# The low half of the weights formed by an accumulating DMA in a two-layer hybrid encoder

## The chip, the cores and the metric

The kernel runs on one core of one Trainium2 chip. The time is the device time in microseconds from the first to the last instruction of one execution. Three runs of the kernel before gave 1634.25, 1635.59 and 1636.38 us; the median is 1635.59.

## What is computed

The reference runs two layers on x of 512 tokens and 1024 channels, all in float32. Cut to its matrix products, one layer is:

```python
h = rmsnorm(x, norm1_g[l])
u = h @ w_in[l]                     # q, k, v, glu_in (two halves), four_in
...
y_a = att.reshape(b, s, WIDTH_A) @ w_proj_a[l]       # differential attention, 8 heads
y_b = jax.nn.silu(cv) @ w_proj_b[l]                  # depthwise convolution of width 31
y_c = fr.reshape(b, s, WIDTH_C) @ w_proj_c[l]        # real part of a 2-D DFT
gates = jax.nn.sigmoid(h @ w_gate[l] + b_gate[l]).reshape(b, s, N_BRANCH, d)
merged = gates[:, :, 0] * y_a + gates[:, :, 1] * y_b + gates[:, :, 2] * y_c
x = x + merged @ w_out[l]
h2 = rmsnorm(x, norm2_g[l])
f_gate, f_up = jnp.split(h2 @ w_ffn_in[l], 2, axis=-1)
x = x + (jax.nn.silu(f_gate) * f_up) @ w_ffn_out[l]
```

## The kernel before

All activations lie with channels on the partitions and the 512 tokens along the row, as tiles of 128 x 512. TensorE multiplies in float32r, a rounded form of float32. To keep the precision, both operands are split into a rounded high half and a low half, the rest that the rounding leaves. A product of a weight tile and an activation tile is then three matmuls: high weight by high activation, high weight by low activation, low weight by high activation (`gemm`, which calls `mm` on line 114, where every matmul is recorded). `split` (from line 144) makes the halves of activations: ScalarE rounds (line 147, or line 150 with a scale), VectorE subtracts (line 148 or 151).

The weights of a layer lie in HBM in the order of their use, cut into 134 chunks of 128 x 1024 (eight tiles of 128 x 128, 512 KB), 268 chunks for both layers. `wtile` hands out one tile after another and calls `chunk` (line 185) for every eighth. `chunk` does the following, all with an early due time (`WL`), so that the scheduler puts it ahead of the work that needs it:

- SyncE loads the chunk into a tile `wr` (line 191), of which there are two buffers;
- ScalarE rounds it into `wh` (line 194), three buffers;
- VectorE subtracts `wh` from `wr` into `wl` (line 195), three buffers.

A scheduler orders the instructions of each engine at build time by these due times and by its own estimate of when each can run; each engine then works through its own list in that order, and semaphores make it wait. An instruction that waits holds up all that stands behind it on its engine. A chunk feeds eight times three matmuls, or in the attention's projections (`qkv`) two steps of four token tiles by three matmuls, where it is the wide operand.

Work that shares the engines with the weights: the convolution on VectorE (line 867, 30 of 31 taps of each of four tiles of a layer), whose tiles GpSimd adds up (line 898, three sums per layer); sums of squares for the norms (ScalarE line 236, GpSimd line 239); the attention's scores (maximum on VectorE line 689, exponential on ScalarE line 691); the merge of the branches (GpSimd line 453); and three loads of DFT tables that GpSimd issues (line 340). The last stage of each layer is the feed-forward part, whose products follow one another without attention between them.

Of the kernel before, what the change touches and what calls it, by code (L numbers as in the profile page):

```python
# [9 lines left out]
F32 = mybir.dt.float32  # L10
F32R = mybir.dt.float32r
I32 = mybir.dt.int32
AF = mybir.ActivationFunctionType
ALU = mybir.AluOpType
# [67 lines left out]
class Hybrid:  # L82
# [102 lines left out]
    def chunk(self, l, c, t):  # L185
        nc = self.nc
        tc = self.tc
        keep = tc.cur_priority
        self.at(t - WL)
        raw = self.wp.tile([P, CHUNK * P], F32, tag="raw", name=self.nm("wr"), bufs=WB[0])  # L190
        nc.sync.dma_start(raw, self.a["w"][l, c])
        hi = self.wp.tile([P, CHUNK * P], F32R, tag="hi", name=self.nm("wh"), bufs=WB[1])
        lo = self.wp.tile([P, CHUNK * P], F32R, tag="lo", name=self.nm("wl"), bufs=WB[2])
        nc.scalar.copy(hi, raw)  # L194
        nc.vector.tensor_tensor(out=lo, in0=raw, in1=hi.bitcast(F32), op=ALU.subtract)  # L195
        tc.cur_priority = keep
        return hi, lo

# [865 lines left out]
```

## Time and profile before

| What | Value |
|---|---|
| median of three runs | 1635.59 us |
| profiled execution, its span | 1635.0 us |
| TensorE busy | 1618.7 us (99%) |
| VectorE busy | 1089.5 us (67%) |
| ScalarE busy | 678.2 us (41%) |
| GpSimd busy | 119.5 us (7%) |
| mean granted TensorE clock | 0.998 |
| read from HBM | 163.30 MB |

The profile is of one execution. Engines are named PE (TensorE), PEld (its loading of the stationary operand), DVE (VectorE), ACT (ScalarE), POOL (GpSimd) and SP (SyncE). A group's row gives line, engine, operation, what it writes from what it reads (buffer numbers left out), shapes and count, then the busy time in us, the mean ns of one, and the idle time of the engine just before, with what ended it. A row of the waits reads: engine and line, what it waited for, us in total, times, longest. A row of the timeline begins with start and duration in us. A row of a window gives its length and each engine's busy time in it. A row of the DMA issues ends with KB each and the median us from issue to landing.

The work is uneven: VectorE is busy nine tenths or more of most of the first 330 us, in which the first layer's convolution and scores run, and about four tenths in the feed-forward stages. TensorE is nearly full everywhere after the first 25 us.

### The profile page before, as it was taken

Reading aid. Unit: us, or ns where it says so; the run is one execution under the profiler, and the core shown is the slowest. Engines: PE = TensorE matmul, PEld = TensorE weight load, DVE = VectorE, ACT = ScalarE, POOL = GpSimd, SP = SyncE. Lnnn points to the kernel's source line nnn. Section 1 sums busy time; section 2 is a strip of 40 time slices with the busy share of each in tenths; the row PEclk is TensorE's granted clock in tenths of the full one; section 3 lists DMA queues with packets and bytes.
Section 4 is the critical chain, followed back from the end, with each engine's and each line's share of the span. In section 5 each row is a group of like instructions: output and inputs, shape, how many; then the busy total and the mean of one; then the engine's idle time right before and its main releaser. Section 6 shows DMA issues by size and latency. Waiting matters only on the chain.

```text
span 1635.0 us, 20023 instructions
## 1 busy us (share of the span) xinstructions
PE 1618.7 (99%) x7512; PEld 1340.8 (82%) x7512; DVE 1089.5 (67%) x1820; ACT 678.2 (41%) x1059; POOL 119.5 (7%) x85
## 2 busy tenths in 40 slices
PE   8999999999999999999999999999999999999999
PEld 6888888887888888888888888888878888888887
DVE  7999999896644433444459999998975444334432
ACT  5345555773443221323344464557634332223221
POOL 4000000112410000000100000001132000000000
PEclk9999999999999999999999999999999999999999
DMA  5545233322432323223343542332224223222332
GB/s 177 176 136 165 78 110 102 98 88 71 136 112 94 103 91 100 93 96 104 128 138 95 162 148 81 100 113 85 87 86 146 95 99 102 92 95 99 93 113 77
DMA packets 61439, 178.50 MB, mean 109 GB/s; under 512 B 8976, under 2 KB 9872, under 8 KB 61344
## 3 DMA queue, kind: packets, MB, share of 16 engines
q1 hardware_dynamic: 60912, 176.11, 33.3%
q0 software_dynamic: 432, 1.13, 0.3%
q8 instruction: 59, 0.97, 0.3%
q14 instruction: 36, 0.29, 0.1%
HBM read 163.30 MB, written 13.89 MB: 108 GB/s over the span
## 4 chain that ended last, share of the span: by engine, by line
PE 96%; ACT 2%; DVE 1%; DMA 0%; issue 0%; SPq 0%; DVEq 0%; ACTq 0%
PE main L114 83%; PE s L114 5%; PE att L114 3%; PE oth L114 3%; PE att L124 2%; DMA V<-in_xT 0%; PE att L583 0%; ACT at L691 0%; ACT cv L924 0%; DVE wl L195 0%; PE oth L124 0%; ACT wh L194 0%; DVE B L151 0%; ACT L924 0%; ACT L441 0%
## 5 line engine op out<-in xcount | busy, mean ns | idle before, releaser
L114 PE MATMUL main<-X,wh 128*128 128x512 f32 x2208 | 692.2, 391 | 0.0
L194 ACT CAST wh<-wr 128x1024 fp32r<-128x1024 f32 x268 | 281.7, 1052 | 649.5 <-PE main L114 375.6
L114 PEld LDWEIGHTS main<-X,wh 128*128 128x128 f32 x2208 | 413.4, 188 | 85.1 <-issue 0.5
L195 DVE TENSOR_TENSOR wl<-wr,wh 128x1024 fp32r<-128x1024 f32 x268 | 341.4, 1274 | 139.4 <-ACT wh L194 138.6
L114 PE MATMUL main<-X,wl 128*128 128x512 f32 x1104 | 431.7, 391 | 0.0
L114 PEld LDWEIGHTS main<-X,wl 128*128 128x128 f32 x1104 | 207.5, 188 | 42.7 <-issue 0.5
L867 DVE SCALAR_TENSOR_TENSOR cv<-cv,hcw,cv 128x497 f32<-128x497 f32 (+14 forms) x240 | 176.4, 735 | 1.2
L114 PE MATMUL main<-att,wh 128*128 128x512 f32 x384 | 119.6, 391 | 3.0 <-ACT att L147 3.0
L691 ACT ACTIVATE at<-s,mx 128x512 f32<-128x512 f32 x128 | 88.0, 688 | 78.6 <-DVE mx L689 63.0
L404 DVE TENSOR_TENSOR M<-main,rb 128x512 f32<-128x512 f32 x42 | 29.1, 692 | 133.8 <-PE main L114 133.8
L114 PE MATMUL main<-A,wh 128*128 128x512 f32 x320 | 106.4, 392 | 0.0
L114 PE MATMUL main<-wh,X 128*128 128x512 f32 x288 | 96.5, 391 | 0.0
L401 DVE TENSOR_TENSOR M<-main,rb 128x512 f32<-128x512 f32 x42 | 29.0, 691 | 91.0 <-PE main L114 91.0
L689 DVE TENSOR_REDUCE mx<-s 128x1 f32<-128x512 f32 x128 | 86.5, 679 | 4.3 <-PE s L114 4.0
L114 PEld LDWEIGHTS main<-att,wh 128*128 128x128 f32 x384 | 71.8, 188 | 19.2 <-ACT att L147 3.5
L114 PE MATMUL main<-act,wh 128*128 128x512 f32 x256 | 80.2, 394 | 0.0
L114 PE MATMUL main<-cv,wh 128*128 128x512 f32 x240 | 77.3, 392 | 1.1 <-ACT cv L147 1.1
L239 POOL TENSOR_TENSOR M<-M,M 128x512 f32<-128x512 f32 x28 | 46.9, 1675 | 421.0 <-ACT M L236 378.3
L114 PE MATMUL main<-att,wl 128*128 128x512 f32 x192 | 75.0, 391 | 0.0
L114 PE MATMUL main<-A,wl 128*128 128x512 f32 x192 | 74.9, 392 | 0.0
L114 PEld LDWEIGHTS main<-A,wh 128*128 128x128 f32 x320 | 59.8, 188 | 12.6 <-issue 0.5
L426 DVE TENSOR_TENSOR V<-main,V 128x512 f32<-128x512 f32 x32 | 22.1, 691 | 65.9 <-PE main L114 65.9
(223 smaller groups left out, 2260.9 us busy)
## 6 DMA issues: line engine op xcount, KB each, us to landing
wr<-in_w SPq DMA_DIRECT2D x268, 512.0 KB, 3.5
dqk<-at SPq DMA_DIRECT2D x32, 256.0 KB, 3.8
qst<-dqk SPq DMA_DIRECT2D x96, 64.0 KB, 1.9
kst<-dqk SPq DMA_DIRECT2D x96, 64.0 KB, 1.9
V<-in_xT SPq DMA_DIRECT2D x8, 256.0 KB, 7.6
att<-dftd SPq DMA_DIRECT2D x8, 256.0 KB, 4.2
M<-in_xT SPq DMA_DIRECT2D x8, 256.0 KB, 3.5
x<-V SPq DMA_DIRECT2D x8, 256.0 KB, 2.6
```

The lines of the kernel that those rows point to most:

```text
L114: return self.pin(self.nc.tensor.matmul(out, lhsT=lhsT, rhs=rhs, start=start, stop=stop))
L124: self.pin(self.nc.tensor.transpose(ps[:, s], src[:, s], self.ident))
L194: nc.scalar.copy(hi, raw)
L195: nc.vector.tensor_tensor(out=lo, in0=raw, in1=hi.bitcast(F32), op=ALU.subtract)
L239: nc.gpsimd.tensor_tensor(out=sq, in0=acc, in1=sq, op=ALU.add)
L401: nc.vector.tensor_tensor(out=z, in0=pg, in1=rb2, op=ALU.mult)
L404: nc.vector.tensor_tensor(out=u, in0=pu, in1=rb2, op=ALU.mult)
L426: nc.vector.tensor_tensor(out=x2[m], in0=ps, in1=x2[m], op=ALU.add)
L689: nc.vector.tensor_reduce(out=mx, in_=ps, axis=AX.X, op=ALU.max, negate=True)
L691: nc.scalar.activation(e, ps, AF.Exp, bias=mx, accum_out=z1 if c else z0)
L867: ins = nc.vector.scalar_tensor_tensor(out=acc[:, a:b], in0=g[:, a + d : b + d], scalar=w[:, t : t + 1], in1=acc[:, a:b], op0=ALU.mult, op ...
```

## The change

The low half no longer comes from a subtraction. ScalarE writes the negated weights into `wl`, rounded by the tile's type, and then GpSimd issues a DMA that reads the same chunk from HBM a second time and adds it onto `wl`. What results is the raw value less its rounded form, as before. ScalarE's rounding into `wh` stays. Lines below 193 keep their numbers, those behind it are one higher: the negation is line 194, the DMA 195, the rounding 196.

```diff
         hi = self.wp.tile([P, CHUNK * P], F32R, tag="hi", name=self.nm("wh"), bufs=WB[1])
         lo = self.wp.tile([P, CHUNK * P], F32R, tag="lo", name=self.nm("wl"), bufs=WB[2])
+        nc.scalar.activation(lo, raw, AF.Copy, scale=-1.0)
+        nc.gpsimd.dma_start(lo, self.a["w"][l, c], accum_op=ALU.add)
         nc.scalar.copy(hi, raw)
-        nc.vector.tensor_tensor(out=lo, in0=raw, in1=hi.bitcast(F32), op=ALU.subtract)
         tc.cur_priority = keep
         return hi, lo
```

The scheduler makes new lists of it. Three places matter below. The first is the start of TensorE's list, the first products of the first layer. A_131 and B_132 are the high and low half of the first activation tile, A_137 and B_138 those of the second; wh_193 and wl_194 are the first chunk, wh_225 and wl_226 the second (wh_224 before). Before:

```order
L114 MATMUL s_190<-A_131,wh_193 128x512
L114 MATMUL s_190<-B_132,wh_193 128x512
L114 MATMUL s_190<-A_131,wl_194 128x512
L114 MATMUL s_190<-A_137,wh_193 128x512
L114 MATMUL s_190<-B_138,wh_193 128x512
L114 MATMUL s_190<-A_137,wl_194 128x512
```

With the change:

```order
L114 MATMUL s_190<-A_131,wh_193 128x512
L114 MATMUL s_190<-B_132,wh_193 128x512
L114 MATMUL s_222<-A_131,wh_225 128x512
L114 MATMUL s_222<-B_132,wh_225 128x512
L114 MATMUL s_190<-A_131,wl_194 128x512
L114 MATMUL s_190<-A_137,wh_193 128x512
L114 MATMUL s_190<-B_138,wh_193 128x512
L114 MATMUL s_190<-A_137,wl_194 128x512
```

Two products with the second chunk's rounded half moved ahead of the first product with a low half.

The second place is GpSimd's list around the sums of the convolution in the first layer. Before, nothing stands between the table loads and the sums:

```order
L340 DMA at_512<-in_dft 128x256
L340 DMA at_522<-in_dft 128x512
L340 DMA at_532<-in_dft 128x512
L898 TENSOR_TENSOR cv_2540<-cv_555,cv_876 128x512
L898 TENSOR_TENSOR cv_2542<-cv_2540,cv_1326 128x512
L898 TENSOR_TENSOR cv_2544<-cv_2542,cv_2056 128x512
```

With the change, from the two chunks ahead of the first sum:

```order
L195 DMA wl_2174<-in_w 128x1024
L195 DMA wl_2244<-in_w 128x1024
L899 TENSOR_TENSOR cv_2573<-cv_564,cv_891 128x512
L899 TENSOR_TENSOR cv_2575<-cv_2573,cv_1347 128x512
L195 DMA wl_2382<-in_w 128x1024
L195 DMA wl_2464<-in_w 128x1024
```

The low halves now share one list with the sums, and a low half behind a sum is issued only after it. At the start of the program the first low half stands ahead of the seven sums of squares (line 240), the second behind three of them, the third behind six and the fourth behind all seven.

The third place is ScalarE's list in the feed-forward part, where the silu (line 402 before) and the rounding of activations (line 147) stand between the chunks. Before:

```order
L194 CAST wh_6099<-wr_6097 128x1024
L402 ACTIVATE M_6056<-M_6056 128x512
L194 CAST wh_6140<-wr_6138 128x1024
L147 CAST act_6062<-M_6059 128x512
L194 CAST wh_6171<-wr_6169 128x1024
```

With the change, at a like stretch:

```order
L196 CAST wh_6431<-wr_6429 128x1024
L194 ACTIVATE wl_6432<-wr_6429 128x1024
L403 ACTIVATE M_6386<-M_6386 128x512
L196 CAST wh_6473<-wr_6471 128x1024
L194 ACTIVATE wl_6474<-wr_6471 128x1024
L147 CAST qst_6392<-M_6389 128x512
L196 CAST wh_6505<-wr_6503 128x1024
L194 ACTIVATE wl_6506<-wr_6503 128x1024
```

The negation stands right behind the rounding of the same chunk. Of the 268 chunks, 241 have this order and 27 the other, negation first; those lie at the start of the program and in the attention's projections of both layers.

TensorE's list of the projections hardly moved: between the last product of wl_632 (the eleventh chunk) and the first of wl_831 (the fourteenth) stand 32 matmuls, and as many between the same chunks before; in the feed-forward part two chunks and two matmuls, 50, lie between.

## The prediction

> **What bounds the kernel now.** I read the page first, for the busy time of each engine.
>
> ```profile
> span 1635.0 us, 20023 instructions
> PE 1618.7 (99%) x7512; PEld 1340.8 (82%) x7512; DVE 1089.5 (67%) x1820; ACT 678.2 (41%) x1059; POOL 119.5 (7%) x85
> ```
>
> TensorE leaves 1635.0 - 1618.7 = 16.3 us of the span unused, so a change that touches no matmul can win at most that. The profiled execution's span of 1635.0 stands 0.6 us under the median of the runs, 1635.59; I carry that 0.6 over. The waits of TensorE say whether the step that is removed ever stood in its way (us in total, times, longest):
>
> ```profile
> PE s L114 <- ACT wh L194: 3.0, 1, 3.0
> PE s L114 <- DVE B L151: 2.3, 2, 1.5
> PEld s L114 <- DVE wl L195: 1.3, 2, 0.8
> ```
>
> The first matmul waits once for a rounded half; the low half is waited for twice, 1.3 us together. Both belong to the start of the program. From there on the low half comes early, and the chain of work that ended last shows it: its longest piece is TensorE alone.
>
> ```profile
> 1281.95 349.40 PE main L114 x1535
> ```
>
> That is 349.40 / 1535 = 0.2276 us per matmul, and 24 matmuls = 5.46 us per chunk of weights. So the question is not what VectorE saves but whether a low half that takes a longer way still arrives in time.
>
> **What goes and what comes.** The two operations per chunk now, 268 of each:
>
> ```profile
> L194 ACT CAST wh<-wr 128x1024 fp32r<-128x1024 f32 x268 | 281.7, 1052 | 649.5 <-PE main L114 375.6 <-issue 200.6 <-PE oth L114 45.6
> L195 DVE TENSOR_TENSOR wl<-wr,wh 128x1024 fp32r<-128x1024 f32 x268 | 341.4, 1274 | 139.4 <-ACT wh L194 138.6
> L147 ACT CAST wth<-att 128x512 fp32r<-128x512 f32 x64 | 37.5, 586 | 40.5 <-PE att L124 40.4
> L150 ACT ACTIVATE A<-V,par 128x512 fp32r<-128x512 f32 x16 | 11.5, 716 | 16.6 <-DVE V L426 14.8 <-DMA V<-in_xT 1.7
> ```
>
> VectorE loses 341.4 us (1089.5 to about 748). Of that only the 1.3 us above lay on TensorE's path, so its worth is at most 1.3 us. ScalarE gains a negating ACTIVATE per chunk. A scaled ACTIVATE costs 716 - 586 = 0.13 us more than a CAST of the same 512 columns, so I take 1.052 + 0.1 = 1.15 us, and 268 x 1.15 = 308 us on top of 678. Its densest stretch has room:
>
> ```profile
> 41.00:164.00 123.00, 123.00 (x583) 102.53 (x583) 117.81 (x242) 59.64 (x99) 0.54 (x1) 1.00 0.49 158
> 287.00:328.00 41.00, 41.00 (x207) 33.71 (x206) 35.65 (x61) 28.95 (x53) 5.91 (x4) 1.00 0.32 95
> ```
>
> (Columns: length, PE, PEld, DVE, ACT, POOL, granted clock, DMA share, GB/s.) In 287 to 328 us ScalarE works 28.95 of 41; about seven chunks more make 37. It is still not full, and I give this nothing, with a bound of some us if its order makes an exponential late. GpSimd issues 268 DMAs more. How long these take is not in the trace, so I bound it by the DMAs that are:
>
> ```profile
> wr<-in_w SPq DMA_DIRECT2D x268, 512.0 KB, 3.5
> qst<-dqk SPq DMA_DIRECT2D x96, 64.0 KB, 1.9
> at<-in_dft POOLq DMA_DIRECT2D x2, 256.0 KB, 3.3
> L340 POOL DMA_DIRECT2D at<-in_dft x3: 536/538/562, 23.1 to 61.9; - x3
> DMA to landing us min/median/max: 3.3/3.5/8.5
> ```
>
> The last line is of the raw weights' loads. GpSimd's own issue takes 0.54 us; 268 x 0.54 = 145 us is no load for an engine that is busy 7%. From 64 to 512 KB a landing grows by 1.6 us, so 448 KB cost 1.6 and 512 KB 1.8. An accumulating DMA has to read its destination too, 512 KB more: 3.5 + 1.8 = 5.3 us from issue to landing. That is my value; the ends are 3.5 (the second read is free) and 8.5 + 1.8 = 10.3 (the slowest raw load, and the read). The Trainium skill's page "Collectives: The Full Stack", section "The bandwidth ceiling: the fold count and why AG ≠ RS ≠ AR", says the DMA engine's add is free and its second source read halves the rate, with about 31 GB/s per engine for a copy; as an estimate by that page 32 KB per engine take 2.1 us in place of 1.1, the landing would be 4.5, and the sum below would lose about 2 us. No run here shows it yet.
>
> The raw weights' two buffers are freed by the last reader, now VectorE and then ScalarE:
>
> ```profile
> SPq L191 <- DVE wl L195: 1100.0, 228, 10.2
> q1 hardware_dynamic: 60912, 176.11, 33.3%
> ```
>
> The reader after the rounding takes 1.15 us in place of 1.27 and is in no queue behind the convolution, so the loads start no later: 0.
>
> **In the steady stages.** The low halves have three buffers, so negation c waits for the last matmul of chunk c-3. Two chunks and two matmuls lie between that and the first use of low half c: 50 x 0.2276 = 11.4 us. That ScalarE starts as soon as TensorE lets go, the end of the program shows:
>
> ```profile
> 1592.63 1.05 ACT L194 CAST wh<-wr 128x1024 fp32r<-128x1024 f32 x1 [4.45 <-PE main L114]
> 1598.16 1.05 ACT L194 CAST wh<-wr 128x1024 fp32r<-128x1024 f32 x1 [4.47 <-PE main L114]
> ```
>
> Here the order puts the negation behind the rounding, so the way is 1.05 + 1.15 + 5.3 = 7.5 us with about 0.2 of handovers: 7.7 of 11.4. The cover of 3.7 us is TensorE's work on the two chunks before, and it is gone when the landing takes over 9.0 us. Cost: 0.
>
> **At the attention's projections.** Where the program changes from one kind of product to the next, the order leaves less. Between the last product of wl_632 and the first of wl_831, three chunks later, stand 32 matmuls, not 50: 7.3 us. Counted through the order, six chunks have 31 to 35 (7.1 to 8.0 us) and seven more 38 to 41. There the negation mostly comes first: 1.15 + 5.3 + 0.2 = 6.7, 0.4 us to spare at the tightest. But four of the six lie in stretches where DMA is busiest (0.49 of the engines at 158 GB/s in 41 to 164 us, as quoted), and each chunk adds 1 MB of reads in 5.46 us, 192 GB/s more. I take 6.5 us there: 1.15 + 6.5 + 0.2 - 7.5 = 0.4 us late, six times, 2.5 us. With 5.3 it is 0; with 8.5 it is about 2.4 us six times and 0.9 seven times, 20 us.
>
> **At the start.** ScalarE and TensorE, and GpSimd's first sums:
>
> ```profile
> 8.38 1.04 ACT L194 CAST wh<-wr 128x1024 fp32r<-128x1024 f32 x1 [3.08 <-DMA wr<-in_w]
> 12.83 1.03 ACT L194 CAST wh<-wr 128x1024 fp32r<-128x1024 f32 x1
> 15.28 0.40 PE L114 MATMUL s<-A,wh 128*128 128x512 f32 x1
> 16.41 0.79 PE L114 MATMUL s<-B,wh 128*128 128x512 f32 x1 [0.73 <-DVE B L151]
> 10.74 12.38 POOL L239 TENSOR_TENSOR M<-M,M 128x512 f32<-128x512 f32 x7 [6.16 <-ACT M L236]
> ```
>
> The first negation stands ahead of the first rounding and the second ahead of the second, and TensorE's order now asks for two products with the second chunk's rounded half (s_222) before it touches the first low half. So TensorE waits until 12.83 + 1.03 + 2 x 1.0 (two negations, whose starts lie about 1 us apart) = 15.9. The row at 15.28 is the tenth product of before; the change has done four by then: six of 0.23 to 0.43 us, 1.4 to 2.6. The wait of 0.73 us for B goes, since VectorE is free. The first low half is issued at 9.5 and lands near 15, inside this wait; only at 10.3 us would it come at 19.8 and add 4. The second stands behind three of GpSimd's sums of 12.38 / 7 = 1.77 us: issue near 17, landing near 22.4, need about 23. I take +1.5 (from -1, all VectorE waits gone, to +6).
>
> **Sum.** 1635.0 + 0 (steady) + 2.5 (projections) + 1.5 (start) = 1639, and 0.6 for what lies around: 1639.6, say **1640**. About 0.2%, 3.3 us, is what a measurement of this kernel can tell from no change, so this lies just above that line.
>
> **Rivals.** *The low half is late everywhere.* If the landing takes over 9.0 us, or the DMA engines cannot do both transfers in 5.46 us, the three buffers turn over too slowly: each us over 9.0 costs a third of a us in each of some 190 chunks that follow one another without attention between. At 10.3 that is 0.43 x 190 = 82, and 1722; at 12 it is 190, and 1830. For it: nothing in the trace accumulates, and the loads on SyncE's queue already hold 33.3% of the engines' time. Against it: the median raw landing is 3.5 us. Chance 0.17.
>
> *GpSimd stands in the way.* Its queue was empty, and now low halves stand behind sums that wait for the convolution.
>
> ```profile
> POOL cv L898 <- DVE cv L867: 507.5, 6, 146.6
> 168.87 1.52 POOL L898 TENSOR_TENSOR cv<-cv,cv 128x512 f32<-128x512 f32 x1 [106.40 <-DVE cv L867]
> 238.01 1.47 POOL L898 TENSOR_TENSOR cv<-cv,cv 128x512 f32<-128x512 f32 x1 [67.61 <-DVE cv L867]
> ```
>
> The order now has the first two sums back to back ahead of wl_2382, so the third tile must be ready about 38 us earlier than 238. Some 30 chunks between 41 and 238 us free 30 x 1.27 = 38 us of VectorE, which is just that. If VectorE does not catch up and is 10 us late, the cover of 3.7 is spent and TensorE stands 6 us, at four such places: 25 us, 1665. It decides from about 3.7 us of lateness. Chance 0.10. The Trainium skill's page "SBUF — State Buffer", section "SBUF: two separate sides", warns of more: GpSimd cannot write a DMA's descriptors while VectorE runs an operation in a two-port mode. What the rows show is a spread of POOL landings of 256 KB and less around 3.3 us while VectorE was 117.81 of 123 us busy, no block of many us; with the block each landing would grow by about one VectorE operation, and the steady cover would still hold it.
>
> *Faster.* VectorE was late at the start, and nothing replaces it: the waits for B (2.3) and wl (1.3) both vanish and the start's six products are won back while B arrives sooner: 1635.6 - 3.6 = 1632. It decides if TensorE is held by B at 15.9 us rather than by rounding. Against it: the order holds TensorE on s_222. Chance 0.08.
>
> **How the numbers follow.** My own case has 0.61 and spreads over the line: half of it under 1639 (start +1, projections 0 to 2), half over. With a little of the two slow rivals small enough not to be seen, within 0.2% gets 0.34; faster 0.08; slower 0.58, of which 0.25 are rivals; the last 0.04 is for what I do not see. The range goes from 1632 (the faster rival) to 1700, which takes in GpSimd's case and the mild part of the late one; about 0.17 is left out.
>
> **What will show it.** Right: wl from an L195 DMA on the GpSimd queue, landing 4.5 to 6.5 us after issue; DVE near 750, ACT near 985; TensorE's chain still one unbroken piece of about 349 us in the last stage; new waits for wl at the start and in the projections, a us or less each. Wrong: PE waiting for wl's DMA in every chunk, a landing over 9 us, or a sum on L899 with TensorE idle behind it.

## The result, and the profile after

The changed kernel took 1683.48 us (median of three runs, 1677.52 to 1685.53) where the kernel before took 1635.59: 1.0286 times as long, interval 1.0259 to 1.0313, or 48 us more. The forecast was 1640, with a range up to 1700.

The head of the page of the changed kernel:

```profile
span 1683.8 us, 20549 instructions
PE 1633.3 (97%) x7512; PEld 1346.1 (80%) x7512; DVE 786.5 (47%) x1552; ACT 921.7 (55%) x1327; POOL 329.7 (20%) x353
```

TensorE's unused time grew from 16.3 to 1683.8 - 1633.3 = 50.5 us, so 34.2 of the 48.7 us by which the span grew are waiting. The other 14.6 are longer busy time (1618.7 to 1633.3) for the same 7512 matmuls. VectorE's subtractions are gone and the others took their work, as intended.

TensorE's waits in the changed kernel (us in total, times, longest):

```profile
PE main L114 <- DMA wl<-in_w: 23.4, 15, 4.7
PE s L114 <- ACT wh L196: 7.2, 2, 4.4
PE main L114 <- ACT A L545: 4.1, 1, 4.1
```

The low half is now the first thing that TensorE waits for, but in 15 places (17 with two single waits of 1.7 us in other rows, 26.8 us in all) and not in 268. The next two rows are waits for ScalarE. Both waits of the second row lie in the first 15 us, and the plain copy below, which loses almost nothing, has them too (8.4 us). Of the third, what kept ScalarE is seen in the DMA rows of the same kernel (queue: packets, MB, share of 16 engines' time; then KB each and median us from issue to landing):

```profile
q0 software_dynamic: 39024, 141.65, 47.3%
q1 hardware_dynamic: 60912, 176.11, 34.8%
...
wr<-in_w SPq DMA_DIRECT2D x268, 512.0 KB, 5.3
wl<-in_w POOLq DMA_DIRECT2D x268, 512.0 KB, 7.7
...
qst<-dqk SPq DMA_DIRECT2D x96, 64.0 KB, 4.5
...
dftd<-at SPq DMA_DIRECT2D x4, 256.0 KB, 8.3
```

A low half lands 7.7 us after its issue. But the raw loads, untouched by the change, take 5.3 in place of 3.5 too, the loads of the scores' operands 4.5 in place of 1.9. The stores of the last row, which the prediction did not show, stood like this in the kernel before:

```profile
dftd<-at SPq DMA_DIRECT2D x4, 256.0 KB, 3.6
```

Where the time went shows in the windows of the changed kernel (length, PE, PEld, DVE, ACT, POOL, granted clock, DMA share, GB/s):

```profile
41.00:164.00 123.00, 113.44 (x495) 91.20 (x494) 94.63 (x209) 67.31 (x99) 17.85 (x22) 0.96 0.86 216
...
600.00:861.00 261.00, 261.00 (x1146) 214.85 (x1145) 50.99 (x73) 116.41 (x135) 49.97 (x55) 1.00 0.91 203
861.00:984.00 123.00, 114.55 (x505) 92.15 (x504) 88.80 (x192) 69.34 (x98) 17.03 (x20) 0.99 0.85 198
```

In the feed-forward stage, 600 to 861 us, TensorE does not miss a moment although the DMA engines are 91% busy. In the other two windows, early in the two layers, it misses 9.6 and 8.5 us of 123, where it missed nothing before; the mean clock is 0.96 in the first of them. The chain of the changed kernel has the unbroken piece of the feed-forward stage as long as before:

```profile
500.10 349.21 PE main L114 x1534
```

Chunk by chunk, the lag of the products behind those of the kernel before (start of the last product with each chunk's low half, in both traces) grew like this, in us. Chunks 0 to 133 are the first layer. The columns on the right are four of the experiments below. Each column is one profiled execution; the three runs of the changed kernel spread over 8 us, so a difference of a us or two between columns says little.

```text
stretch (chunks)                      after   half tiles  control  traffic only  small after
start (up to 0)                        +3.7      +1.2       +0.2        0.0         +3.4
first products (0-8)                   +0.4       0.0       +1.1       +2.1         -0.2
attention's projections (8-20)        +14.0      +6.7       -0.7       +8.4        +17.3
beside the scores (20-44)             +11.9     +12.8       -0.1       +5.3        +17.4
end of attention (44-60)               -6.6      -8.1      +10.2      +12.8         -1.5
merge, feed-forward (60-130)           +1.8       0.0       +0.5       +0.5         +1.3
second layer, first products (-142)    +3.3       0.0        0.0       +2.3         +4.7
its projections (142-154)              +8.7      +5.0       +0.1       +1.8        +10.2
beside its scores (154-176)           +16.0     +13.8       -4.1       +5.4        +14.4
its end of attention (176-192)         -7.4      -7.6      +15.3      +11.6         -4.0
the rest (192-266)                     +2.8       0.0       +0.3       +0.5         +4.1
at the end of the span                 48.7      23.9       22.6       50.7         67.1
```

The gain at the end of attention is for the most part no time won back. The new order puts part of the attention's own work earlier: up to the last product of chunk 44 TensorE has run 32 instructions more than before (26 up to chunk 176), and by chunks 60 and 192 the two orders are level again. The plain copy below has the same order on TensorE, instruction for instruction, and shows +6.3 and -8.0 us in the two stretches of the first layer, +7.3 and -7.6 in the second. So these two rows are to be read together: 5.3 and 8.6 us net in the changed kernel.

The largest single step of the changed kernel, 10.8 us between chunks 8 and 12, can be followed in SyncE's list (start, duration, line, transfer):

```profile
70.91 0.92 SPq L347 DMA_DIRECT2D dftd<-at  x2
80.35 0.32 SPq L755 DMA_DIRECT2D att<-dftd  x1
80.72 0.57 SPq L191 DMA_DIRECT2D wr<-in_w  x1
```

A table load that reads back what was just stored (L755) stands ahead of the raw load (L191). The second store ends its issue at 71.83, and SyncE stands still for 8.5 us until 80.35; the raw load behind it starts at 80.72. Before, the same wait was 2.6 us:

```profile
68.43 0.91 SPq L346 DMA_DIRECT2D dftd<-at  x2
71.95 0.32 SPq L754 DMA_DIRECT2D att<-dftd  x1
72.32 0.42 SPq L191 DMA_DIRECT2D wr<-in_w  x1
```

Then ScalarE, in the changed kernel, waits for that raw tile:

```profile
87.87 1.06 ACT L194 ACTIVATE wl<-wr 128x1024 fp32r<-128x1024 f32 x1 [8.40 <-DMA wr<-in_w]
88.83 1.03 ACT L196 CAST wh<-wr 128x1024 fp32r<-128x1024 f32 x1
89.76 0.58 ACT L545 COPY A<-main 128x512 f32<-128x512 f32 x1
```

The copy on L545 needs no weight at all, it empties a bank of TensorE, but it stands behind the negation. TensorE, waiting for that bank and then for the low half:

```profile
90.39 0.50 PE L114 MATMUL main<-wh,X 128*128 128x512 f32 x1 [4.12 <-ACT A L545]
...
95.73 0.80 PE L114 MATMUL main<-wl,X 128*128 128x512 f32 x1 [2.88 <-DMA wl<-in_w]
96.32 1.05 PE L114 MATMUL main<-wh,X 128*128 128x512 f32 x2
```

The last row is another part of the loss: two matmuls take 1.05 us where two take 0.61 in an undisturbed stretch. Short windows of the changed kernel around that gap and a later one show a low mean clock; from 91.47 to 101.71 and from 924.32 to 927.74 us it is 0.50:

```profile
90.00:103.00 13.00, 9.73 (x27) 7.23 (x28) 9.82 (x31) 8.27 (x15) 0.91 (x2) 0.61 0.80 208
...
924.00:928.00 4.00, 4.00 (x12) 3.14 (x11) 4.00 (x18) 0.96 (x3) 0.00 (x0) 0.57 0.49 164
```

### The profile page after: what moved, and what is told of

Read it like the earlier page. It is cut to its first block, busy times and chain, and to the rows that moved or that the text cites. A ratio compares the mean times of both kernels' runs of the same rounds, so it can differ in the third digit from the quotient of the medians.

```text
span 1683.8 us, 20549 instructions
## 1 busy us (share of the span) xinstructions
PE 1633.3 (97%) x7512; PEld 1346.1 (80%) x7512; DVE 786.5 (47%) x1552; ACT 921.7 (55%) x1327; POOL 329.7 (20%) x353
## 3 DMA queue, kind: packets, MB, share of 16 engines
q0 software_dynamic: 39024, 141.65, 47.3%
q1 hardware_dynamic: 60912, 176.11, 34.8%
HBM read 303.81 MB, written 13.89 MB: 189 GB/s over the span
## 4 chain that ended last, share of the span: by engine, by line
PE 70%; issue 13%; DMA 7%; DVE 4%; ACT 3%; POOL 3%; SPq 0%; POOLq 0%; ACTq 0%; DVEq 0%
PE main L114 63%; DMA wl<-in_w 4%; PE s L114 3%; POOL wl L195 2%; PE att L114 1%; DMA wr<-in_w 1%; DVE cv L868 1%; PE att L124 1%; PE oth L114 1%; ACT wl L194 1%; DVE mx L690 1%; POOL M L240 1%; ACT wh L196 1%; ACT at L692 1%; DVE at L697 0%
## 5 line engine op out<-in xcount | busy, mean ns | idle before, releaser
L195 POOL DMA_DIRECT2D wl<-in_w x268 | 229.7, 857 | 1217.5 <-ACT wl L194 1189.3
L194 ACT ACTIVATE wl<-wr 128x1024 fp32r<-128x1024 f32 x268 | 282.3, 1054 | 59.5 <-DMA wr<-in_w 33.6
L868 DVE SCALAR_TENSOR_TENSOR cv<-cv,hcw,cv 128x497 f32<-128x497 f32 (+14 forms) x240 | 181.8, 758 | 2.3
L114 PE MATMUL main<-wh,X 128*128 128x512 f32 x288 | 100.9, 408 | 4.1 <-ACT A L545 4.1
L114 PE MATMUL main<-wl,X 128*128 128x512 f32 x144 | 59.7, 414 | 11.8 <-DMA wl<-in_w 11.7
```

What stands on the lines that cost most here:

```text
L114: return self.pin(self.nc.tensor.matmul(out, lhsT=lhsT, rhs=rhs, start=start, stop=stop))
L194: nc.scalar.activation(lo, raw, AF.Copy, scale=-1.0)
L195: nc.gpsimd.dma_start(lo, self.a["w"][l, c], accum_op=ALU.add)
L868: ins = nc.vector.scalar_tensor_tensor(out=acc[:, a:b], in0=g[:, a + d : b + d], scalar=w[:, t : t + 1], in1=acc[:, a:b], op0=ALU.mult, op ...
```

## The experiments

After the result I held theory A: the low half lands late wherever the order leaves less than about 10 us for it. The rivals: the load that the doubled reading puts on the DMA engines delays raw loads and table traffic (B), or ScalarE's new work does it (C). Each text on record spells out its own theories.

**Negation without the second DMA.** ScalarE still negates, VectorE adds the raw tile. The work on ScalarE is that of the change; GpSimd and DMA do nothing new.

```diff
-        nc.gpsimd.dma_start(lo, self.a["w"][l, c], accum_op=ALU.add)
+        nc.vector.tensor_tensor(out=lo, in0=raw, in1=lo.bitcast(F32), op=ALU.add)
```

> Keeps the negation on ScalarE, but VectorE adds the raw weights onto it and no second DMA runs. Theory A (late arrivals: the second transfer of each chunk makes all landings longer, the low half's 7.7 us and the raw load's 5.3 us, and TensorE idles where the order leaves 7 to 9 us): 1634 to 1640 us. Theory B (ScalarE's 282 us of negations make its list late): 1665 to 1685 us. Theory C (GpSimd's list, sums and table loads ahead of low halves): as A, since GpSimd's list is that of before.

Measured: 1652.05 us, ratio 1.0097 (1.0081 to 1.0112), between what the theories expected. The loss is not where the changed kernel loses: up to chunk 56 this kernel was 0.7 to 6.5 us ahead of the kernel before, then it lost 10.2 us in one spot of the first layer and 6.9 in one of the second.

```profile
PE oth L124 <- ACT at L181: 7.6, 2, 3.8
```

That is a scaling on ScalarE that TensorE waits for there. The changed kernel does not have this wait. So this run says that ScalarE's negations are harmless in the places that matter here; it doesn't say what they cost in the changed kernel's own order, which the next run does.

**Plain copy.** The same list and the same two loads of each chunk, but the DMA overwrites and does not add: the low half is then the raw weight, and the subtraction is left out.

```diff
-        nc.gpsimd.dma_start(lo, self.a["w"][l, c], accum_op=ALU.add)
+        nc.gpsimd.dma_start(lo, self.a["w"][l, c])
```

> The same DMA from GpSimd's list as a plain copy, so the destination is not read (the low half is then the raw weight itself, which leaves out the addition). Theory A: packets of 4096 B take about 159 ns and not 328, the low half lands in 4.5 to 5.5 us and the raw load in about 4, time 1640 to 1660 us. Theory B: ScalarE has the same work, so 1675 to 1685 us. Theory C: GpSimd's list is the same, 1670 to 1685 us.

Measured: 1639.02 us, ratio 1.0021 (1.0012 to 1.0031). Nearly all of the loss is gone, a little more than theory A expected, with ScalarE's work, GpSimd's place in the way and the doubled HBM reading (303.81 MB) all still there. What differs is on the DMA side of this kernel (the last row, the stores of tables, is nearly as in the changed kernel):

```profile
q1 hardware_dynamic: 60912, 176.11, 31.4%
q0 software_dynamic: 39024, 141.65, 24.8%
...
wr<-in_w SPq DMA_DIRECT2D x268, 512.0 KB, 3.5
wl<-in_w POOLq DMA_DIRECT2D x268, 512.0 KB, 4.5
...
dftd<-at SPq DMA_DIRECT2D x4, 256.0 KB, 7.6
```

The same 39024 packets of q0 took 0.248 x 16 x 1636.6 / 39024 = 0.166 us each here and 0.473 x 16 x 1683.8 / 39024 = 0.327 us with the addition: 1.96 times as long. The Trainium skill's page "Collectives: The Full Stack", section "The bandwidth ceiling: the fold count and why AG ≠ RS ≠ AR", says of the reduce step of a ReduceScatter that the addition costs nothing but a second source read, which halves the rate; the 1.96 agrees with that. In the traces the first packet of a low half runs 2.8 us (median) after its issue and its packets take 4.5 us with the addition, 2.2 and 2.0 without. The issue on GpSimd is dearer as well: 857 ns in the changed kernel, 536 here.

```profile
L195 POOL DMA_DIRECT2D wl<-in_w x268 | 143.5, 536 | 1245.1 <-ACT wl L194 1230.0
```

So the accumulation is the cause, and neither ScalarE nor the second load by itself. Late table stores are not enough either: at the place followed above SyncE stands still for 5.6 us in this kernel, and it loses 0.7 us between chunks 8 and 12. The order covers that much. In the changed kernel it was 8.5 us, and the raw tile behind it took another 7.1. Whether the accumulation works through the late low half or through the load was still open.

**Where it is paid.** The DMA only from chunk 60 of each layer on (merge and feed-forward), the old subtraction ahead of it; and the other way round.

```diff
+        if c >= 60:
         nc.scalar.activation(lo, raw, AF.Copy, scale=-1.0)
         nc.gpsimd.dma_start(lo, self.a["w"][l, c], accum_op=ALU.add)
         nc.scalar.copy(hi, raw)
+        else:
+            nc.scalar.copy(hi, raw)
+            nc.vector.tensor_tensor(out=lo, in0=raw, in1=hi.bitcast(F32), op=ALU.subtract)
```

> The accumulating DMA only for chunks 60 to 133 of each layer (output projection and feed-forward part), the subtraction on VectorE for the first 60. Theory A: the steady stages have 11.4 us for a way of about 10 us and cost nothing, 1634 to 1640 us. If the DMA as such slowed TensorE everywhere (a rival), about half of the 48 us would stay, 1655 to 1662 us.

> The reverse: the accumulating DMA for the first 60 chunks of each layer, the subtraction for the rest. Theory A: the whole loss, 1676 to 1686 us. The rival of a slow-down everywhere: 1655 to 1662 us.

Measured: 1643.68 us, ratio 1.0045 (1.0029 to 1.0062), with the DMA in the back part, and 1679.03, ratio 1.0258 (1.0232 to 1.0285), with the DMA in front. The 148 chunks behind cost 8 us, nearly all at the change into them (3.8 between chunks 59 and 63, 3 between 192 and 204), and the 120 in front cost 43. The expectation for the back part was a little too good: TensorE waits there for low halves in six places, 5.4 us in all.

**One raw buffer more, one rounded buffer fewer.**

```diff
-WB = (2, 3, 3)
+WB = (3, 2, 3)
```

> The change with three buffers for the raw weights, two for the rounded half and three for the low half, so that a raw load can start one chunk (5.5 us) earlier and the low half's lead stays at 8 to 11 us. If late raw loads (5.3 us to landing, and held on SyncE's list behind other loads) make most of the loss: 1642 to 1655 us. If the low half's own way of about 10 us does: 1665 to 1680 us.

Measured: 1669.57 us, ratio 1.0201 (1.0187 to 1.0215). These buffers give back 14 us; the step between chunks 8 and 12 fell from 10.8 to 6.2 us. That is in the range of the low half as the main cause. How much of the 14 is due to raw loads that may start earlier is not shown, since the order changed too: in this kernel the negation stands ahead of its chunk's rounding at all 268 chunks, in place of 27, so the low half is on its way a us sooner.

**A fourth low half**, with a control that gives the kernel before the same buffers.

```diff
-WB = (2, 3, 3)
+WB = (2, 2, 4)
```

> The change with four buffers for the low half, two for the rounded half and two for the raw weights (as much memory as before). The least lead after the start grows from about 7 to about 10 us and the usual one from 11 to 14 or 17. If the low half's own way of about 10 us makes most of the loss: 1636 to 1646 us. If late raw loads do: 1665 to 1680 us. If two buffers of the rounded half are too few, it shows as waits of TensorE on L196, and the same in the control c1.

> Control: the kernel before, subtraction on VectorE, with the buffers of e7 (raw 2, rounded 2, low 4). If the buffers matter only for the long way of the DMA: 1634 to 1639 us. If two buffers of the rounded half cost something: over 1640 us.

Measured: 2052.04 us, ratio 1.2548 (1.2528 to 1.2568), and 1644.28 for the control, 1.0047 (1.0033 to 1.0061). So two rounded buffers cost the kernel before some 8 us. Nobody expected the first figure. ScalarE's list of this kernel says why: with two low buffers more than rounded ones, the negation of the next chunk stands ahead of a rounding, at 207 of the 268 chunks.

```text
L194 ACTIVATE wl_5886<-wr_5883 128x1024
L194 ACTIVATE wl_5918<-wr_5915 128x1024
L196 CAST wh_5885<-wr_5883 128x1024
```

Here wl_5918 belongs to the next chunk, whose raw tile may still be on its way, and the rounding of a tile that is there waits behind it. The waits of this kernel:

```profile
ACT wl L194 <- DMA wr<-in_w: 1012.4, 225, 8.7
PE main L114 <- ACT wh L196: 170.0, 88, 4.1
```

The run therefore tells nothing about a fourth low half. It tells what an in-order engine costs that waits for a load ahead of a job that is ready.

**Two DMAs per chunk**, 512 columns each, onto the same tile.

```diff
-        nc.gpsimd.dma_start(lo, self.a["w"][l, c], accum_op=ALU.add)
+        for s in (slice(0, T), slice(T, 2 * T)):
+            nc.gpsimd.dma_start(lo[:, s], self.a["w"][l, c][:, s], accum_op=ALU.add)
```

> The change with the accumulating DMA cut into two of 512 columns. If the landing is made of the packets (8 of 328 ns per engine), the first half lands about 1.3 us sooner and the thin places lose less: 1660 to 1675 us. If it is made of GpSimd's preparation (first packet about 2.7 us after the issue), two issues per chunk make the second half later than before: 1684 to 1710 us.

Measured: 1666.67 us, ratio 1.0183 (1.0169 to 1.0197): 17 us better than one DMA, though GpSimd issues twice as often. The landing rows of this kernel:

```profile
wr<-in_w SPq DMA_DIRECT2D x268, 512.0 KB, 4.8
wl<-in_w POOLq DMA_DIRECT2D x536, 256.0 KB, 6.6
```

Half of the bytes save 1.1 of 7.7 us, near the 1.3 that the expectation had for the packets, and the time is in its range too; the dearer preparation did not decide. TensorE's waits for low halves fell from 23.4 us to 15.6 and the raw landing from 5.3 to 4.8, so this run does not say which of the two gave the 17 us.

**Half tiles.** Each half of a low half in a tile of its own, six buffers in the same memory, so that a half can be asked for ten products earlier.

```diff
-        lo = self.wp.tile([P, CHUNK * P], F32R, tag="lo", name=self.nm("wl"), bufs=WB[2])
-        nc.scalar.activation(lo, raw, AF.Copy, scale=-1.0)
-        nc.gpsimd.dma_start(lo, self.a["w"][l, c], accum_op=ALU.add)
+        lo = []
+        for s in (slice(0, T), slice(T, 2 * T)):
+            x = self.wp.tile([P, T], F32R, tag="lo", name=self.nm("wl"), bufs=2 * WB[2])
+            nc.scalar.activation(x, raw[:, s], AF.Copy, scale=-1.0)
+            nc.gpsimd.dma_start(x, self.a["w"][l, c][:, s], accum_op=ALU.add)
+            lo.append(x)
```

> The change with each low half kept in two tiles of 512 columns (six buffers, the same memory): each half is negated, added to by a DMA of its own and given back by itself, so the first half of a tile is asked for ten products earlier in the list (60 products of 0.2276 us, 13.7 us, and not 11.4) and is 256 KB instead of 512. Theory A (what is lost is the time by which low halves come later than the lead that the list leaves them): most of it comes back, 1642 to 1658, below the two-DMA kernel without tiles of their own (1667). Theory B (what is lost is the load on the DMA engines, which makes raw loads and table stores late whatever the low half waits for): as the two-DMA kernel, 1662 to 1672. Theory C (the second issue on GpSimd and the second negation on ScalarE cost more than the lead gives): above 1672.

Measured: 1662.69 us, ratio 1.0168 (1.0146 to 1.0190), the lower end of what B gives and not what A gives. TensorE's waits of this kernel make it the most telling run of all:

```profile
PE s L114 <- ACT at L696: 8.6, 5, 3.3
PE s L114 <- ACT wh L199: 7.5, 2, 4.7
PE main L114 <- ACT A L549: 4.5, 1, 4.5
PE main L114 <- DMA wl<-in_w: 2.7, 2, 2.5
```

The wait for low halves is down from 23.4 us to 2.7, and still the kernel stands 26 us above the one before. What is left are mostly waits for ScalarE (the second row again at the start), and ScalarE of this kernel waited for raw tiles (before: 5.2 us, twice; in the changed kernel: 48.4 us in 14 places, so the half tiles' own order adds to it):

```profile
ACT wl L196 <- DMA wr<-in_w: 89.7, 41, 7.7
```

The longest of them, in the timelines of ScalarE and of TensorE:

```profile
976.99 0.63 ACT L196 ACTIVATE wl<-wr 128x512 fp32r<-128x512 f32 x1 [7.68 <-DMA wr<-in_w]
...
981.40 0.69 ACT L696 ACTIVATE at<-s,mx 128x512 f32<-128x512 f32 x1
```

```profile
982.23 0.50 PE L114 MATMUL s<-kst,qst 96*128 96x512 f32 x1 [3.29 <-ACT at L696]
```

A raw tile comes late, the negation waits for it, the exponential of the scores stands behind the negation (with four other operations and a table load of 1.28 us between them), and the next score product waits for the bank that the exponential empties.

**The load alone.** All the traffic of the change, and no product that waits for it. VectorE subtracts as before; beside it ScalarE negates the rounded half into a spare tile, GpSimd's DMA adds the raw weights onto that, and nobody reads it. The spare tiles need 8 KB of each partition, which come from one rounded buffer, one tile `at` and one `ar`; a control has these smaller buffers without the traffic, and a third kernel is the change itself in them.

```diff
-WB = (2, 3, 3)
+WB = (2, 2, 3)
...
-"cv": 8, "at": 5, "ar": 2,
+"cv": 8, "at": 4, "ar": 1,
...
         nc.vector.tensor_tensor(out=lo, in0=raw, in1=hi.bitcast(F32), op=ALU.subtract)
+        z = self.wp.tile([P, CHUNK * P], F32R, tag="z", name=self.nm("wz"), bufs=2)
+        nc.scalar.activation(z, hi.bitcast(F32), AF.Copy, scale=-1.0)
+        nc.gpsimd.dma_start(z, self.a["w"][l, c], accum_op=ALU.add)
```

> The kernel before with 8 KB less of buffers (two rounded halves instead of three, four tiles at instead of five, one ar instead of two): the control of the next two, which need that room. With two rounded and four low halves the kernel before took 1644. Every theory: 1640 to 1660.

> The control with all the traffic of the change and none of its dependency: VectorE subtracts as before, and beside it ScalarE negates the rounded half into a spare tile (two buffers) onto which GpSimd's DMA adds the raw weights; nobody reads the spare tile. Theory A (products wait for low halves that land late): within 6 us of the control. Theory B (the doubled reading slows the raw loads and the table traffic, which would delay the products whoever makes the low half): 20 to 45 us above the control. If raw landings grow to about 5 us here as well, and the time doesn't, the load alone is harmless.

> The change with the control's buffers: the traffic of the kernel before it in this list, and the dependency too. Every theory: 30 to 60 us above the control. What it is above the traffic-only kernel is what the wait for the landing costs; what the traffic-only kernel is above the control is what the load costs.

Measured: control 1658.75 us, ratio 1.0137 (1.0122 to 1.0152); traffic only 1683.33, 1.0275 (1.0251 to 1.0299); the change in these buffers 1705.16, 1.0424 (1.0406 to 1.0442). So the traffic that nobody reads costs 24.6 us over the control, as B said (20 to 45), and the change itself comes to 21.8 more. The landings in the traffic-only kernel are those of the changed one:

```profile
wr<-in_w SPq DMA_DIRECT2D x268, 512.0 KB, 5.4
wz<-in_w POOLq DMA_DIRECT2D x268, 512.0 KB, 7.7
```

ScalarE waits 115.2 us for raw tiles in it:

```profile
ACT wh L194 <- DMA wr<-in_w: 115.2, 36, 8.2
```

In the control that row reads:

```profile
ACT wh L194 <- DMA wr<-in_w: 3.0, 1, 3.0
```

TensorE's share of it shows in its own waits: 7.0 us in four places for the 64 KB loads of a score operand, which it never waited for in the control.

Some things have to be kept in mind with the split. The traffic is not quite free of a dependency, since ScalarE has to wait until a spare tile has landed before it may write it again:

```profile
ACT wz L197 <- DMA wz<-in_w: 15.3, 15, 2.7
```

The control and the traffic-only kernel both have the stall at the end of attention that the first experiment had, and the third kernel does not have it, so the dependency's share of 21.8 is rather too low than too high: the two stretches of the table read +10 to +15 us in two columns and a small gain in the third. The third kernel also has its negations ahead of the roundings, at all 268 chunks, as the kernel with three raw buffers. The traffic-only kernel also has ScalarE's 268 negations, which the control lacks. The plain copy has them too and lost next to nothing, but its list is another one. So 24.6 us is the price of the traffic together with these negations and waits.

## Why the prediction was right in sign and too small

The forecast was slower by a little, 4 us, and slower is what came, by ten times as much. That the time lies in the range is luck: the range reached up to 1700 for the sake of the two slow rivals, and neither of them is what happened. Point by point:

- *The removed subtraction is worth at most 1.3 us.* Nothing speaks against it. The plain copy, which also drops it, wins nothing.
- *The landing, 5.3 us (3.5 to 10.3).* Too small: 7.7. The term rested on a plain load of 3.5 us with nothing else under way, and added 1.8 for the second read. The plain copy shows what a second load beside the raw one takes, 4.5. The accumulation then added 3.2 and not 1.8: about 0.6 before the first packet and 2.5 while the packets run. The estimate of 4.5, worked out from the Trainium skill's page "Collectives: The Full Stack", was further off still, though the halved rate of that page is what the packets show.
- *Steady stages, 0.* Right, and it held up under the wrong landing: 0.2 + 1.05 + 1.05 + 7.7 = 10.0 us of the 11.4 that the order leaves. The chain's piece of 349.21 us beside 349.40 is what the prediction named as the sign for it. The rival of a low half that is late everywhere, which needed a landing over 9.0 us, is refuted too.
- *Projections, 2.5 us.* Failed in size: 14.0 us (with the tables beside them) and 8.7. The prediction's own sum with the measured landing and negation gives (1.05 + 7.7 + 0.2 - 7.5) x 6 = 8.7 us, and it had named 20 for a landing of 8.5; what came in both layers together is 22.7. So the landing explains part, and not all of it came by that way: the half tiles, with almost no wait for low halves, still lost 6.7 and 5.0 us in the two stretches, and the traffic-only kernel 8.4 and 1.8.
- *"The loads start no later: 0."* This is the step that failed outright. It asked who frees the raw buffers, and not what the loads meet in the DMA engines or in SyncE's list. Raw tiles landed after 5.3 us in place of 3.5, and some were issued late behind tables that had to make a round trip. The traffic-only kernel puts a price on it: some 25 us, half of the whole loss, with the reservations above.
- *The scores.* They had no term beyond "a bound of some us". With the end of attention, where the orders are level again, the stretches lost 5.3 and 8.6 us. The half tiles, which lost 4.7 and 6.2 there, show one way: exponentials stand behind negations on ScalarE, and these wait for raw tiles.
- *The start, 1.5 us (-1 to +6).* 3.7, inside the bounds. The first low half, issued at 8.52 us, took 8.9 to land, and TensorE, ready for it at 15.8, waited for it until 17.5; the prediction had it land inside another wait.
- *GpSimd behind the convolution's sums.* It did not happen by that way. The wait was 507.5 us before and is now

```profile
POOL cv L899 <- DVE cv L868: 37.4, 2, 19.5
```

  In both layers TensorE does wait for the low half behind the second sum, 2.13 us at 235.86 and 4.71 at 1063.64, its longest wait for a low half:

```profile
1054.16 0.86 POOL L195 DMA_DIRECT2D wl<-in_w  x1 [2.35 <-ACT wl L194]
1063.64 0.79 PE L114 MATMUL main<-A,wl 128*128 128x512 f32 x1 [4.71 <-DMA wl<-in_w]
```

  But GpSimd had done with the sum 2.35 us before it could issue, and waited for ScalarE's negation. So ScalarE's list and a landing of 9.4 us made this low half late, not the sum. (The landings that the prediction read beside a busy VectorE are thin evidence: of the three table loads only the one at 61.9 us lies in that window.)
- *The clock.* Not foreseen: 14.6 of the 48.7 us are longer busy time. In the stretches at half the clock TensorE was busy for 25.7 us, and for 6.7 in the kernel before, so the clock accounts for (25.7 - 6.7) / 2 = 9.5 of them; the other 5 are not explained.
- *VectorE near 750 and ScalarE near 985.* The page says 786.5 and 921.7. A negation took 1.054 us and not 1.15. The rest is in how the page counts: back-to-back instructions overlap a little, and an overlap counts once, so that removing 341.4 us of rows took 303.0 off the page, and adding 282.3 put 243.5 on it.

What stays open: how the loss divides exactly between the late low half and the load. The smaller buffers give 24.6 to 21.8; the half tiles give 21 us for the late low half (1683.5 to 1662.7) and 26 for the rest, but two smaller DMAs without tiles of their own had already won 17 of these 21. That both shares are near half is as far as the runs go. A late raw tile also makes the low half late, so the two are not separate to the end. A fourth low half with three rounded ones was not tried.

None of the variants of the change came below the kernel before, so there is none to recommend.

## What to carry to other kernels

A transfer that replaces an operation has two prices: its own latency against the lead that the order leaves it, and what its load does to every other transfer; the second was about half of the bill here and appears in no row of the new instruction. Ask for each load that shares the DMA engines what stands behind it in an in-order list, on the issuing engine and on the engine that consumes it, since jobs that never touch the transfer (a bank to be emptied, an exponential) wait there too. The stages with a regular rhythm can take such a change for nothing while changes of stage pay for it, so price the tight places one by one. When two kernels are compared place by place, check that their orders have done the same work up to there.

## What the runs showed of the hardware

An accumulating DMA from GpSimd took 857 ns to issue where a plain one took 536, and 0.327 us per packet where a plain one took 0.166. With both transfers of each chunk the DMA engines were busy 82% of the span (47.3 + 34.8) and a 512 KB raw load took 5.3 us in place of 3.5; with the plain copy the engines were busy 56% and it stayed at 3.5. The 256 KB stores of tables took 7.6 us there already, where they took 3.6 before and 8.3 with the addition.

A gap of TensorE can cost more than its length:

```profile
923.10 0.50 PE L114 MATMUL main<-wl,X 128*128 128x512 f32 x1 [3.13 <-DMA wl<-in_w]
```

From 924.32 to 927.74 us the clock was 0.50, so this gap cost about 3.1 + 3.4 / 2 = 4.8 us. The Trainium skill's page "TensorE: Matmul & The Clock Gate", section "What's actually happening", has the clock fall to half after an idle window of about 3.4 us and come back after one of work. The length of this slow stretch agrees. But the fall came here after shorter gaps: after the 3.13 us above, and in the two windows below, where TensorE was busy 2.47 of 4 us, with no gap over 1.53, and then ran 3 us at 0.51.

```profile
204.00:208.00 4.00, 2.47 (x20) 2.17 (x19) 4.00 (x5) 2.26 (x6) 1.70 (x2) 0.94 0.86 192
208.00:211.00 3.00, 3.00 (x15) 2.90 (x15) 3.00 (x8) 1.15 (x3) 0.00 (x0) 0.51 0.50 100
```
